# Rotating 32 x 3 images by 90 degrees: one group of four slabs in 32 KB rows, and a first transfer of 1 MB

## The chip, the cores and the metric

The kernel runs on one core of a Trainium2 chip. The metric is the device time of one execution in microseconds (us): 123.2 us before the change, the median of three runs (122.94 to 123.29).

## The reference

```python
def setup_inputs():
    batch, c, h, w = 32, 3, 256, 256
    return {"x": np.random.randn(batch, c, h, w).astype(np.float32)}

def reference(x):
    return np.rot90(x, k=-1, axes=(-2, -1)).astype(np.float32)
```

Each of the 96 images of 256 x 256 floats is turned clockwise: out[i, j] = x[255 - j, i]. Nothing is calculated; 25.17 MB are read, rearranged and written.

## The kernel before

The input is seen as 24,576 rows of 256 floats (1 KB each), `rows_in`; the output likewise, `rows_out`. A **slab** is 2,048 rows, 8 images, 2 MB: 128 partitions times 16 rows. There are 12 slabs, and they are kept in six **pairs** of 4 MB. Each pair has its own tile `u` of 32 KB per partition, so all 24 MB lie in SBUF at once (192 KB per partition) and no buffer is used twice.

**Loads.** All go out from SP's queue, in program order, before any store. Pair 0 comes as two transfers of 2 MB, one per slab (line 55), each partition getting two rows of 8 KB; slab 1 is loaded first. Pairs 1 to 5 come as two transfers each (line 59), for every second partition: 64 partitions with two rows of 16 KB, one from each half of the pair, 2 MB apart in memory.

**Turning.** VectorE (DVE) transposes blocks of 32 x 32 elements, 2048 elements per partition to an instruction; access patterns on both sides do the rest of the rotation, negative steps included. A pair is turned in place. Since an instruction would overwrite what another has not read yet, `turn_pair` cuts the pair into four quarters (low and high half of the columns, low and high half of the rows): the first quarter is written to `spare[n % 2]`, one of two tiles in PSUM (line 78); the other three are written into the places that the quarter before set free (line 82); then ScalarE (ACT) copies the first quarter from `spare` to the place that is left, in two copies (line 84). Pair 0 has another layout: slab 1 is turned into both `spare` tiles, slab 0 into slab 1's place (`turn_slab`, line 65), and ACT copies the `spare` tiles into slab 0's place (line 70).

**Stores.** Two transfers of 2 MB for each pair (line 97), each from every second partition, in rows of 16 KB. They go out from SP's queue as well, so each one stands behind all the loads and behind the stores of the pairs before it.

The order of the work is set by the data: the framework puts in the semaphore waits. A transfer also waits for an earlier one whose semaphore it takes over (eight are in use). PSUM is read and written by DVE and ACT alone.

Of the kernel before, what the change touches and what calls it, by code (L numbers as in the profile page):

```python
# [1 line left out]

# [4 lines left out]


@with_exitstack  # L10
def kernel(
    ctx: ExitStack,
    tc: tile.TileContext,
    x: bass.AP,
    out: bass.AP,
):

    nc = tc.nc
    fp32 = mybir.dt.float32

    B, C, H, W = x.shape
    P = nc.NUM_PARTITIONS
    R = 16
    I = 2  # L30
    E = R * W
    n_slabs = B * C * H // (P * R)
    hw = R // 2

    rows_in = x.rearrange("b c h w -> (b c h) w")
    rows_out = out.rearrange("b c h w -> (b c h) w")

    def short(rows):
        return rows.rearrange("(n i p r) w -> n p i (r w)", i=I, p=P, r=R // I)

    def long(rows):
        return rows.rearrange("(n a i m r) w -> n i m a (r w)", a=2, i=I, m=P // I, r=R)

    ld_short, ld_long, st_long = short(rows_in), long(rows_in), long(rows_out)

    pairs = [
        ctx.enter_context(tc.tile_pool(name=f"pair{n}", bufs=1)).tile([P, 2, E], fp32, name=f"u{n}")
        for n in range(n_slabs // 2)
    ]
    psum = ctx.enter_context(tc.tile_pool(name="psum", bufs=1, space=bass.MemoryType.PSUM))  # L50
    spare = [psum.tile([P, E // 2], fp32, name=f"spare{h}") for h in range(2)]


    for s, home in ((1, 0), (0, 1)):
        nc.sync.dma_start(
            out=pairs[0][:, home].rearrange("p (i f) -> p i f", i=I), in_=ld_short[s])
    for n in range(1, len(pairs)):
        for i in range(I):
            nc.sync.dma_start(out=pairs[n][i::I], in_=ld_long[n, i])

    def turn_slab(src, dsts):
        s = src.rearrange("p (i r g c) -> p c r g i", i=I, r=R // I, c=R)
        for h, d in enumerate(dsts):
            d = d.rearrange("p (c k r) -> p c r k", c=hw, r=R // I)[:, :, ::-1, ::-1]
            nc.vector.transpose(out=d, in_=s[:, h * hw : (h + 1) * hw])  # L65

    turn_slab(pairs[0][:, 0], spare)
    turn_slab(pairs[0][:, 1], [pairs[0][:, 0, : E // 2], pairs[0][:, 0, E // 2 :]])
    for h in range(2):
        nc.scalar.copy(out=pairs[0][:, 1, h * E // 2 : (h + 1) * E // 2], in_=spare[h])  # L70

    def turn_pair(n):
        u = pairs[n]
        src = u.rearrange("p a (r g c) -> p c r g a", r=R, c=R)
        dst = u.rearrange("p i (c k r) -> p c r k i", c=R, r=R)[:, :, ::-1, ::-1, :]
        held = spare[n % 2]
        low, high = slice(0, hw), slice(hw, R)
        nc.vector.transpose(  # L78
            out=held.rearrange("p (i c k r) -> p c r k i", i=I, c=hw, r=hw)[:, :, ::-1, ::-1, :],
            in_=src[:, low, low])  # L80
        for c, r in ((low, high), (high, high), (high, low)):
            nc.vector.transpose(out=dst[:, c, r], in_=src[:, c, r])  # L82
        for i in range(I):
            nc.scalar.copy(  # L84
                out=u[:, i, : E // 2].rearrange("p (c r) -> p c r", r=R)[:, :, hw:],
                in_=held[:, i * E // 4 : (i + 1) * E // 4].rearrange("p (c r) -> p c r", r=hw))

    for n in range(1, len(pairs)):
        turn_pair(n)
    for n in range(len(pairs)):  # L90
        for a in range(2):
            if n == 0:

                st = rows_out[: 2 * P * R].rearrange("(s i m r) w -> i m s (r w)", s=2, i=I, r=R)[a]
            else:
                st = rows_out.rearrange("(n a i m r) w -> n a m i (r w)", a=2, i=I, m=P // I, r=R)[n, a]
            nc.sync.dma_start(out=st, in_=pairs[n][a::2])


# [1 line left out]
_INS = ['x']  # L101
_OUTS = [((32, 3, 256, 256), 'float32')]


# [23 lines left out]
```

## Time and profile before

The profiled execution took 122.98 us, of which 121.2 us are the span that the profile shows.

| what | value |
|---|---|
| median of three runs | 123.2 us |
| profiled execution | 122.98 us |
| its span | 121.2 us |
| data moved | 50.33 MB, mean 415 GB/s over the span |
| transfers | 12 loads and 12 stores, 2 MB each |
| DVE, ACT busy | 86.6 us, 14.5 us |
| last store issued | 101.14 to 103.11 us (two issues) |

The lines of groups give: code line, engine, operation, target <- source with partitions x elements and type, count, then total busy time, mean duration of one in ns, and after the second bar the idle time of the engine before them with what ended most of it. Slices are forty equal parts of the span; the DMA digits are the mean busy share of the 16 DMA engines in tenths (9 is 90% or more). Lines of stretches give the window, its length, busy time of DVE, ACT and POOL with counts, the clock of TensorE (not used here), DMA share and GB/s.

### The profile page before, as it was taken

To read this page: it belongs to the slowest core of one execution; us is meant where nothing else is said; L and a number is where in the kernel's file an instruction comes from. 1 tells how busy PE (TensorE), PEld (TensorE's weight loads), DVE (VectorE), ACT (ScalarE), POOL (GpSimd) and SP (SyncE) were. 2 spreads that over 40 slices of the span, in tenths; PEclk is the share of its full clock that TensorE was granted. 3 is DMA by queue.
4 is the path that set the end of the run, shared out by engine and by line. 5 is a ranking of instruction groups with operands and counts; after the bars stand their busy time and mean duration, and the time that the engine had idled before them with its cause. 6 is when DMAs were issued, how large, how long until landed. Compare 5 with 4: busy or idle time off the path is not lost.

```text
span 121.2 us, 125 instructions
## 1 busy us (share of the span) xinstructions
DVE 86.6 (71%) x24; ACT 14.5 (12%) x13; POOL 0.2 (0%) x4
## 2 busy tenths in 40 slices
DVE  0029999619999999999999999999999970000000
ACT  0000400380000330005000060000600023000000
POOL 0000000000000000000000000000000000000000
DMA  4999999999999999999999999999999999999994
GB/s 87 403 419 433 465 433 433 427 427 433 433 411 422 416 427 433 433 433 433 422 433 433 433 433 433 433 433 433 433 433 433 433 427 427 433 433 433 433 433 184
DMA packets 3713, 50.33 MB, mean 415 GB/s; under 512 B 385, under 2 KB 385, under 8 KB 385
## 3 DMA queue, kind: packets, MB, share of 16 engines
q1 hardware_dynamic: 3712, 50.33, 97.9%
q14 instruction: 1, 0.00, 0.0%
HBM read 25.17 MB, written 25.17 MB: 415 GB/s over the span
## 4 chain that ended last, share of the span: by engine, by line
DVE 60%; issue 13%; DMA 6%; ACT 2%; ACTq 1%
DVE u L82 33%; DVE spare L78 15%; DVE u L65 6%; DMA u<-in_x_dram 6%; DVE spare L65 6%; ACT u L70 2%; ACT u L84 1%; ACTq L123 1%
## 5 line engine op out<-in xcount | busy, mean ns | idle before, releaser
L82 DVE STREAM_TRANSPOSE u<-u 128x2048 f32<-128x2048 f32 x15 | 54.3, 3619 | 0.5
L78 DVE STREAM_TRANSPOSE spare<-u 128x2048 f32<-128x2048 f32 x5 | 17.9, 3574 | 3.7 <-ACT u L70 3.7
L84 ACT COPY u<-spare 128x1024 f32<-128x1024 f32 x10 | 9.6, 1014 | 64.6 <-DVE u L82 64.6
L65 DVE STREAM_TRANSPOSE spare<-u 128x2048 f32<-128x2048 f32 x2 | 7.1, 3585 | 8.3 <-DMA u<-in_x_dram 8.3
L65 DVE STREAM_TRANSPOSE u<-u 128x2048 f32<-128x2048 f32 x2 | 7.8, 3986 | 0.0
L70 ACT COPY u<-spare 128x2048 f32<-128x2048 f32 x2 | 3.6, 1869 | 8.7 <-DVE u L65 8.7
L70 ACT ACT_TABLE_LOAD x1 | 1.3, 1283 | 13.3 <-DMA u<-in_x_dram 13.3
L112 POOL MEMSET const-bfloat16-1.0<- 128x1 bf16 x1 | 0.1, 101 | 0.0
L112 POOL MEMSET const-uint8-127<- 128x1 uint8 x1 | 0.1, 101 | 0.0
L112 POOL MEMSET const-float32-0.0<- 128x1 f32 x1 | 0.1, 98 | 0.2 <-issue 0.2
L112 POOL MEMSET const-float32-1.0<- 128x1 f32 x1 | 0.1, 98 | 0.0
## 6 DMA issues: line engine op xcount, KB each, us to landing
u<-in_x_dram SPq DMA_DIRECT2D x12, 2048.0 KB, 31.1
out_dram<-u SPq DMA_DIRECT2D x12, 2048.0 KB, 28.3
```

The source lines that it names most:

```text
L65: nc.vector.transpose(out=d, in_=s[:, h * hw : (h + 1) * hw])
L70: nc.scalar.copy(out=pairs[0][:, 1, h * E // 2 : (h + 1) * E // 2], in_=spare[h])
L78: nc.vector.transpose(out=held.rearrange("p (i c k r) -> p c r k i", i=I, c=hw, r=hw)[:, :, ::-1, ::-1, :], in_=src[:, low, low])
L82: nc.vector.transpose(out=dst[:, c, r], in_=src[:, c, r])
L84: nc.scalar.copy(out=u[:, i, : E // 2].rearrange("p (c r) -> p c r", r=R)[:, :, hw:], in_=held[:, i * E // 4 : (i + 1) * E // 4].rearrange ...
L112: nc = _bacc.Bacc("TRN2", target_bir_lowering=False, num_devices=1)
L123: with _tile.TileContext(nc) as tc:
```

## The change

- The six pairs become five **groups** of 2, 2, 4, 2 and 2 slabs (`sizes`). The group of four is one tile of 64 KB per partition.
- Group 0 is loaded in three transfers instead of two: slab 1 in two of 1 MB, each with one row of 8 KB per partition, then slab 0 in one of 2 MB as before.
- A group with `I` slabs is loaded in `I` transfers of 2 MB, each for every `I`-th partition. For the group of four this means 32 partitions with two rows of 32 KB, which lie 4 MB apart in memory. The groups of two are loaded as before.
- `turn_pair` becomes `turn_group`. With four slabs each quarter is turned by `T` = 2 instructions of 2048 elements, so the group has eight transpositions, two of them into both `spare` tiles, and its quarter is copied back by eight copies of 512 elements (two `spare` tiles, four slabs). In place, each instruction now writes to four places 16 KB apart.
- The first quarter of group 1 goes to a new tile `extra` in SBUF (8 KB per partition); the group of four uses both `spare` tiles, group 3 `spare[0]` and group 4 `spare[1]`.
- The stores keep their size and shape: 2 MB from every second partition, in rows of 16 KB. The group of four has four of them, for its first two slabs and then for its last two.

```diff
     nc = tc.nc
     fp32 = mybir.dt.float32
     B, C, H, W = x.shape
     P = nc.NUM_PARTITIONS
     R = 16
-    I = 2
     E = R * W
-    n_slabs = B * C * H // (P * R)
     hw = R // 2
+    low, high = slice(0, hw), slice(hw, R)
     rows_in = x.rearrange("b c h w -> (b c h) w")
     rows_out = out.rearrange("b c h w -> (b c h) w")
-    def short(rows):
-        return rows.rearrange("(n i p r) w -> n p i (r w)", i=I, p=P, r=R // I)
-
-    def long(rows):
-        return rows.rearrange("(n a i m r) w -> n i m a (r w)", a=2, i=I, m=P // I, r=R)
-
-    ld_short, ld_long, st_long = short(rows_in), long(rows_in), long(rows_out)
-
-    pairs = [
-        ctx.enter_context(tc.tile_pool(name=f"pair{n}", bufs=1)).tile([P, 2, E], fp32, name=f"u{n}")
-        for n in range(n_slabs // 2)
+    sizes = (2, 2, 4, 2, 2)
+    first = [sum(sizes[:n]) for n in range(len(sizes))]
+    groups = [
+        ctx.enter_context(tc.tile_pool(name=f"group{n}", bufs=1)).tile([P, s, E], fp32, name=f"u{n}")
+        for n, s in enumerate(sizes)
     ]
     psum = ctx.enter_context(tc.tile_pool(name="psum", bufs=1, space=bass.MemoryType.PSUM))
     spare = [psum.tile([P, E // 2], fp32, name=f"spare{h}") for h in range(2)]
+    extra = ctx.enter_context(tc.tile_pool(name="extra", bufs=1)).tile([P, E // 2], fp32, name="extra")
+
+    def rows_of(rows, n):
+        return rows[first[n] * P * R : (first[n] + sizes[n]) * P * R]
-    for s, home in ((1, 0), (0, 1)):
-        nc.sync.dma_start(
-            out=pairs[0][:, home].rearrange("p (i f) -> p i f", i=I), in_=ld_short[s])
-    for n in range(1, len(pairs)):
+    ld = rows_of(rows_in, 0).rearrange("(s i p r) w -> s i p (r w)", s=2, i=2, p=P)
+    home = [groups[0][:, s].rearrange("p (i f) -> p i f", i=2) for s in range(2)]
+    for i in range(2):
+        nc.sync.dma_start(out=home[0][:, i], in_=ld[1, i])
+    nc.sync.dma_start(out=home[1], in_=ld[0].transpose([1, 0, 2]))
+    for n in range(1, len(sizes)):
+        I = sizes[n]
+        ld = rows_of(rows_in, n).rearrange("(a i m r) w -> i m a (r w)", a=2, i=I, m=P // I)
         for i in range(I):
-            nc.sync.dma_start(out=pairs[n][i::I], in_=ld_long[n, i])
+            nc.sync.dma_start(
+                out=groups[n].rearrange("p s f -> p (s f)").rearrange("p (a f) -> p a f", a=2)[i::I],
+                in_=ld[i])
     def turn_slab(src, dsts):
-        s = src.rearrange("p (i r g c) -> p c r g i", i=I, r=R // I, c=R)
+        s = src.rearrange("p (i r g c) -> p c r g i", i=2, r=R // 2, c=R)
         for h, d in enumerate(dsts):
-            d = d.rearrange("p (c k r) -> p c r k", c=hw, r=R // I)[:, :, ::-1, ::-1]
+            d = d.rearrange("p (c k r) -> p c r k", c=hw, r=R // 2)[:, :, ::-1, ::-1]
             nc.vector.transpose(out=d, in_=s[:, h * hw : (h + 1) * hw])
-    turn_slab(pairs[0][:, 0], spare)
-    turn_slab(pairs[0][:, 1], [pairs[0][:, 0, : E // 2], pairs[0][:, 0, E // 2 :]])
+    u = groups[0]
+    turn_slab(u[:, 0], spare)
+    turn_slab(u[:, 1], [u[:, 0, : E // 2], u[:, 0, E // 2 :]])
     for h in range(2):
-        nc.scalar.copy(out=pairs[0][:, 1, h * E // 2 : (h + 1) * E // 2], in_=spare[h])
+        nc.scalar.copy(out=u[:, 1, h * E // 2 : (h + 1) * E // 2], in_=spare[h])
-    def turn_pair(n):
-        u = pairs[n]
-        src = u.rearrange("p a (r g c) -> p c r g a", r=R, c=R)
-        dst = u.rearrange("p i (c k r) -> p c r k i", c=R, r=R)[:, :, ::-1, ::-1, :]
-        held = spare[n % 2]
-        low, high = slice(0, hw), slice(hw, R)
-        nc.vector.transpose(
-            out=held.rearrange("p (i c k r) -> p c r k i", i=I, c=hw, r=hw)[:, :, ::-1, ::-1, :],
-            in_=src[:, low, low])
+    def turn_group(n, held):
+        I = sizes[n]
+        T = I // 2
+        K = W // (R * T)
+        u = groups[n].rearrange("p s f -> p (s f)")
+        src = u.rearrange("p (a t r g c) -> p t c r g a", a=2, t=T, r=R, c=R)
+        dst = u.rearrange("p (i c k t r) -> p t c r k i", i=I, c=R, k=K, t=T)[:, ::-1, :, ::-1, ::-1, :]
+        for t in range(T):
+            nc.vector.transpose(
+                out=held[t].rearrange("p (i c k r) -> p c r k i", i=I, c=hw, k=K)[:, :, ::-1, ::-1, :],
+                in_=src[:, t, low, low])
         for c, r in ((low, high), (high, high), (high, low)):
-            nc.vector.transpose(out=dst[:, c, r], in_=src[:, c, r])
-        for i in range(I):
-            nc.scalar.copy(
-                out=u[:, i, : E // 2].rearrange("p (c r) -> p c r", r=R)[:, :, hw:],
-                in_=held[:, i * E // 4 : (i + 1) * E // 4].rearrange("p (c r) -> p c r", r=hw))
+            for t in range(T):
+                nc.vector.transpose(out=dst[:, t, c, r], in_=src[:, t, c, r])
+        back = u.rearrange("p (i c k t r) -> p t i c k r", i=I, c=R, k=K, t=T)[:, ::-1]
+        for t in range(T):
+            kept = held[t].rearrange("p (i c k r) -> p i c k r", i=I, c=hw, k=K)
+            for i in range(I):
+                nc.scalar.copy(out=back[:, t, i, low, :, high], in_=kept[:, i])
-    for n in range(1, len(pairs)):
-        turn_pair(n)
-    for n in range(len(pairs)):
-        for a in range(2):
-            if n == 0:
+    for n, held in enumerate(([extra], spare, [spare[0]], [spare[1]]), 1):
+        turn_group(n, held)
-                st = rows_out[: 2 * P * R].rearrange("(s i m r) w -> i m s (r w)", s=2, i=I, r=R)[a]
-            else:
-                st = rows_out.rearrange("(n a i m r) w -> n a m i (r w)", a=2, i=I, m=P // I, r=R)[n, a]
-            nc.sync.dma_start(out=st, in_=pairs[n][a::2])
+
+    st = rows_of(rows_out, 0).rearrange("(s i m r) w -> i m s (r w)", s=2, i=2, m=P // 2)
+    for a in range(2):
+        nc.sync.dma_start(out=st[a], in_=groups[0][a::2])
+    for n in range(1, len(sizes)):
+        st = rows_of(rows_out, n).rearrange("(a i m r) w -> a m i (r w)", a=2, i=sizes[n], m=P // 2)
+        for i in range(0, sizes[n], 2):
+            for a in range(2):
+                nc.sync.dma_start(out=st[a][:, i : i + 2], in_=groups[n][a::2, i : i + 2])
```

## The prediction

> **What bounds the kernel now.** I read the page's head and its forty slices first, then the groups by line, then the waits, then stretches of the DMA stream.
>
> ```profile
> span 121.2 us, 125 instructions
> DVE 86.6 (71%) x24; ACT 14.5 (12%) x13; POOL 0.2 (0%) x4
> DMA  4999999999999999999999999999999999999994
> GB/s 87 403 419 433 465 433 433 427 427 433 433 411 422 416 427 433 433 433 433 422 433 433 433 433 433 433 433 433 433 433 433 433 427 427 433 433 433 433 433 184
> q1 hardware_dynamic: 3712, 50.33, 97.9%
> ```
>
> One queue keeps the 16 DMA engines busy for 97.9% of the span: only the first and the last slice have gaps. DVE is busy for 71%. The chain of waits names DVE for 60% of the span, but it ends when the last store is issued, at 103 us, and the data of that store waits in the queue for some 17 us more. So the bytes set the end: 25.17 MB in, then 25.17 MB out, in one unbroken line. Three things can move the time: the unfilled start, the rate, and a hole in the line.
>
> ```profile
> 0.00:2.00 2.00, 0.00 (x0) 0.00 (x0) 0.20 (x4) 1.00 0.20 29
> 5.00:12.00 7.00, 3.74 (x2) 0.00 (x0) 0.00 (x0) 1.00 1.01 428
> 14.00:57.00 43.00, 39.06 (x12) 7.20 (x7) 0.00 (x0) 1.00 1.01 428
> 62.00:118.00 56.00, 36.88 (x11) 5.78 (x6) 0.00 (x0) 1.00 1.01 433
> 119.90:121.20 1.30, 0.00 (x0) 0.00 (x0) 0.00 (x0) 1.00 0.00 0
> ```
>
> The last two columns are DMA share and GB/s. Loads in 8 KB rows (5 to 12 us) run at 428, loads in 16 KB rows (14 to 57) at 428, stores in 16 KB rows at 433. No data moves after 119.9. Counted back from there, the stores of the last four of the six pairs (16.78 MB at 433 = 38.8) begin at 81.1 us.
>
> ```profile
> L82 DVE STREAM_TRANSPOSE u<-u 128x2048 f32<-128x2048 f32 x15 | 54.3, 3619 | 0.5
> L78 DVE STREAM_TRANSPOSE spare<-u 128x2048 f32<-128x2048 f32 x5 | 17.9, 3574 | 3.7 <-ACT u L70 3.7
> L84 ACT COPY u<-spare 128x1024 f32<-128x1024 f32 x10 | 9.6, 1014 | 64.6 <-DVE u L82 64.6
> L65 DVE STREAM_TRANSPOSE u<-u 128x2048 f32<-128x2048 f32 x2 | 7.8, 3986 | 0.0
> L70 ACT COPY u<-spare 128x2048 f32<-128x2048 f32 x2 | 3.6, 1869 | 8.7 <-DVE u L65 8.7
> 13.27 1.28 ACT L70 ACT_TABLE_LOAD   x1 [13.27 <-DMA u<-in_x_dram]
> 23.23 3.63 ACT L70 COPY u<-spare 128x2048 f32<-128x2048 f32 x2 [8.67 <-DVE u L65]
> SPq L59 <- DMA u<-in_x_dram: 15.4, 4, 4.3
> ```
>
> The same 2048 elements per partition take 3619 ns written in place by L82 and 3986 ns by L65: the write pattern matters, by 10%.
>
> **The change part by part.** The sum is made on the profiled execution, 122.98 us: its span of 121.2 and 1.78 around it. That is 0.2 under the median of 123.2; at the end I carry the difference over to the median.
>
> *32 KB rows.* The 8.39 MB of the large group come in 256 rows instead of 512. At 428 they take 19.60 us. Bounds: the stores' 433 would make it 19.37, a gain of 0.23; the nearest step, from 8 to 16 KB rows, changed 428 into 428, a gain of nothing. A loss is not excluded, since each load now spans 32 partitions and its rows lie in two places 4 MB apart, not 2: the worst slice of loads past the start ran at 411, which makes it 20.41, a loss of 0.81. I take a gain of 0.10, between the two near rows.
>
> A rule of the Trainium skill speaks against this part: in "DMA: Bandwidth & Descriptors", section "Latency and other measured facts", copies lose rate when partitions step through HBM by large powers of two (164 GB/s at a 2 MiB pitch, 103 at 4 MiB). The pitch between this kernel's two rows per partition is 2 MB, and its loads run at 428 all the same. If the rule held for the step from 2 to 4 MB, the group would load at 428 x 103/164 = 269 and take 31.2 us, 11.6 longer, an estimate from that page; I go by the row.
>
> *The first transfer.* Before, 2 MB in 256 rows; after, 1 MB in 128, then 1 MB, then 2 MB: the same bytes, one more issue.
>
> ```profile
> 1.70:1.80 0.10, 0.00 (x0) 0.00 (x0) 0.00 (x0) 1.00 0.00 0
> 1.80:1.90 0.10, 0.00 (x0) 0.00 (x0) 0.00 (x0) 1.00 0.87 164
> 2.20:2.30 0.10, 0.00 (x0) 0.00 (x0) 0.00 (x0) 1.00 0.70 164
> 2.30:2.50 0.20, 0.00 (x0) 0.00 (x0) 0.00 (x0) 1.00 0.00 0
> 3.00:4.00 1.00, 0.00 (x0) 0.00 (x0) 0.00 (x0) 1.00 0.91 377
> ```
>
> The engines' first rows are spread over 1.8 to 2.3 us, and the full rate comes later. In this stretch and its neighbours 1.05 MB moved from 1.7 to 5.0; at 428 that takes 2.45 us, so the start wastes 0.85. This is the upper bound of the gain. If the spread of 0.5 us comes from handing out 256 rows, half the rows make it 0.25, and I take that gain. The other bound: nothing is gained, and the extra issue costs one issue of L55 (442 ns in the median). That issue is hidden, since 1 MB keeps the engines busy for 2.45 us; with that cover gone it would cost 0.44. On SP it delays the eleven loads behind it by 0.44, all of which already queue far ahead of the data. The first transposition still needs both halves of its slab, so DVE starts at about 8.2 as now.
>
> *SP.* Four loads now wait for an earlier landing (the last row of the groups above: the ninth to twelfth wait for the first to fourth). With thirteen loads five wait, and their first landings come earlier, after 1 MB. Stores keep their order behind all loads; every group's store stands behind the group before it, so one late group holds up all later ones.
>
> *DVE and ACT, and whether the line of stores stays closed.* Pair 0 is unchanged and ends at 23.20. The second group holds its first quarter in `extra`, so the wait of 3.7 us for L70's copies is gone: off the path, worth nothing, because next comes the large group, which needs four loads. They land at 13.27 + 12.58 MB / 428 = 42.7. The second group ends by 23.2 + 3.57 to 3.99 (its first write goes to SBUF now) + 3 x 3.62 = 38.1 at the latest, so DVE then idles for some 5 us. The large group: 2 x 3.57 + 6 x 3.62 = 28.9, ending at 71.6. Its copies: 2048 elements took 1869 ns and 1024 took 1014, so 0.835 ns each and 159 fixed; eight of 512 elements take 587 each, 4.7 together. All done at 76.3; by the code's order the first store needs six of them, 75.1. First data of a transfer came 0.97 after its issue began (0.73 to 1.70) and an issue of a store lasts 0.6; with 1.6 for both, on the safe side, store data is ready by 77.9 against 81.1 when the line would run dry. The margin is 3.2 us.
>
> The third large step: the next group's first write needs `spare[0]` free, that is, four copies, 2.4 us of DVE idle: 71.6 + 2.4 + 14.4 = 88.4, plus 2 copies 90.4, needed at 81.1 + 19.4 = 100.5. The last group: 102.8 plus copies 104.8, needed at 110.2. Both are covered, by some 8 and 4 us after the issue.
>
> What the trace doesn't show is the large group's write pattern: four places 16 KB apart, 128 bytes between neighbours, where L82 had two places and 64 bytes. Nearest rows: 3.57 and 3.99. At 3.99 the six in-place steps add 2.2 and the margin is still 1.0. So this part costs nothing, covered by the queue of stores.
>
> The Trainium skill's page "SBUF — State Buffer" ("Door 1: The DMA port swizzle") says that each access that crosses into another 16-byte line pays. All of these strides cross at every element, so by it they cost the same 3.62; the 3986 beside 3619 shows that the stride does matter here, and I keep 3.99 as the upper row.
>
> *Sum:* 122.98 - 0.10 - 0.25 = 122.63 for the profiled execution, a change of -0.35; on the median 122.85.
>
> **The rivals.**
>
> *A hole in the stores* (the slower side). If the eight transpositions of the large group take over 3.2 / 8 = 0.40 more each (4.0 in place), the engines run dry at 81 us, and each 0.1 beyond costs 0.8. For it: L65's 3986 lies just under that bound, and the pattern has wider strides than any seen. Against: L82's pattern already jumps 16 KB at every element and runs at 3619. With twice L65's excess, 0.74 each: 5.9 - 3.2 = 2.7, less the 0.35: 125.5.
>
> *The 32 KB rows load slower.* At 411: +0.81 - 0.25: 123.8. For it: only 32 partitions per transfer. Against: 128 and 64 partitions ran at the same 428.
>
> *Nothing arrives.* The rows are cut into 16 KB packets, or gain nothing, and the start is ruled by the first reads and not by the row count: 123.2. For it: 8 and 16 KB rows show one rate, and the later issues with 128 rows took longer (606 ns) than the first two with 256 (442).
>
> *The start is mended in full:* -0.85 - 0.10: 122.25.
>
> **How the numbers follow.** Forecast 0.50, its own range 122.5 to 123.1; hole 0.17; slower rows 0.08; nothing 0.18; start in full 0.07. About 0.3%, 0.37 us or 122.83 on the median, is what a measurement of this kernel can tell from no change. The forecast lies on that line: I give 0.30 of it to faster and 0.20 to same. With the full start faster has 0.37; rounded up for gains in both parts at once, 0.40. Same: 0.20 + 0.18 less that share, 0.35. Slower: hole and slower rows, 0.25. The range goes from 122.4 to 124.2: below lies most of the full start, above most of the hole.
>
> **What would show it.** Right: 256 fewer packets in the queue's line (not counting those of the one transfer more); the first rows spread over less than 0.5 us and the first 1 MB moved before 4.8; 428 or more between 23 and 42 us; DVE idle for about 5 us before the large group; no slice under 420 around 81 us; the last data at about 119.5. Wrong: in-place steps of the large group over 4.0 us with a dip of the DMA share near 81 (the hole), or a lower rate between 23 and 42 (slower rows).

## The result, and the profile after

The changed kernel took 123.5 us in the median of 21 runs (123.21 to 123.75), the kernel before 123.1 in as many (122.85 to 123.43). The ratio is 1.0034, 95% interval 1.0026 to 1.0042: slower by 0.4 us. The profiled execution of the changed kernel took 123.44 us with a span of 121.6.

The head of the page after, with the forty slices and the queue:

```profile
span 121.6 us, 130 instructions
DVE 87.4 (72%) x24; ACT 14.9 (12%) x17; POOL 0.2 (0%) x4
DMA  4999999998989899999999999999999999999993
GB/s 92 423 426 434 442 431 431 436 506 356 506 356 506 350 431 431 426 431 431 377 409 431 431 431 431 442 431 431 431 431 442 431 436 431 431 431 431 431 431 135
q1 hardware_dynamic: 3472, 50.33, 97.7%
```

The packets fell from 3712 to 3472: 256 rows fewer, and 16 completions more for the one transfer more. So the 32 KB rows are really moved as such. The 506 and 356 in turn from 24 to 42 us are these rows, whose bytes are counted where a row begins. Two slices stand out that have no counterpart before: 377 and 409, from 58 to 64 us. There the last load ends and the first store begins. I call this place **the turn**. The same stretches as before, with DMA share and GB/s last:

```profile
5.00:12.00 7.00, 3.88 (x2) 0.00 (x0) 0.00 (x0) 1.00 1.00 421
23.00:41.00 18.00, 14.91 (x5) 5.63 (x4) 0.00 (x0) 1.00 1.01 437
59.00:61.00 2.00, 2.00 (x2) 0.00 (x0) 0.00 (x0) 1.00 0.99 328
61.00:63.00 2.00, 2.00 (x1) 0.00 (x0) 0.00 (x0) 1.00 0.95 393
62.00:118.00 56.00, 38.06 (x11) 7.96 (x12) 0.00 (x0) 1.00 1.01 433
```

And the same stretches around the turn in the kernel before:

```profile
59.00:61.00 2.00, 1.97 (x2) 0.00 (x0) 0.00 (x0) 1.00 1.03 426
61.00:63.00 2.00, 2.00 (x1) 0.00 (x0) 0.00 (x0) 1.00 0.98 418
```

The share stays near 1 while the rate falls to 328: the engines are busy, and each packet takes longer (up to 1265 ns for 16 KB, where 611 to 615 is the rule). This is no hole. DVE and ACT by time, at the places that the prediction spoke of:

```profile
22.90 3.90 DVE L85 STREAM_TRANSPOSE extra<-u 128x2048 f32<-128x2048 f32 x1
42.29 7.08 DVE L85 STREAM_TRANSPOSE spare<-u 128x2048 f32<-128x2048 f32 x2 [4.28 <-DMA u<-in_x_dram]
49.40 21.91 DVE L90 STREAM_TRANSPOSE u<-u 128x2048 f32<-128x2048 f32 x6
71.34 3.03 ACT L95 COPY u<-spare 128x512 f32<-128x512 f32 x6 [2.68 <-DVE u L90]
72.94 3.61 DVE L85 STREAM_TRANSPOSE spare<-u 128x2048 f32<-128x2048 f32 x1 [1.63 <-ACT u L95]
```

The large group starts at 42.29 (42.7 was forecast), its six steps in place take 21.91 / 6 = 3.65 each, and its copies end at 74.4. The forecast's side of DVE and ACT holds within 2 us, and the line of stores is closed: 433 GB/s from 62 to 118.

**Where the 0.4 us went.** Windows of 2 us are too coarse for tenths, since a packet counts whole where it begins. The trace's packet records are finer: each transfer leaves 16 short packets of 4 bytes, one by each DMA engine, which I call its completions. The time from one transfer's completions to the next repeats to some ns while nothing changes. Worked out from these records (us; mean of the 16 engines, and the last engine; "second profile" is that of the changed kernel run again, below):

```
                               before     after      after, second profile
2 MB load, 16 KB rows           4.893      4.894      4.894      mean
2 MB load, 32 KB rows            -         4.855      4.857      mean
2 MB store                      4.862      4.862      4.862      mean
first data start at             1.82       1.74       1.73
first 2 MB complete at          7.64       7.49       7.50       mean
last load (the turn), mean      4.95       5.45       5.37
last load (the turn), last      4.89       5.65       5.53
spread of the 16 before it      0.56       0.45       0.53
last completion of all        120.06     120.44     120.39
```

The start is 0.15 us ahead, and four loads of the large group save 4 x 0.037 = 0.15 more. The last load then takes 0.50 us longer than before on the mean and 0.76 on the last engine (0.42 and 0.64 in the second profile). From there to the end every store takes 4.862 in both kernels. On the mean this makes -0.15 - 0.15 + 0.50 = +0.20 (0.18 by the completions of the last store); the last completion is 0.38 later, since the engines also stand further apart after the turn (0.82 us against 0.36) and the last of them sets the end. So in both profiles of the changed kernel the whole loss arises in one transfer, the last load, at the turn. Of the kernel before there is one profile.

### The profile page after: what moved, and what is told of

The parts are those of the page before. It is cut to its first block, busy times and chain, and to the rows that moved or that the text cites. A ratio compares the mean times of both kernels' runs of the same rounds, so it can differ in the third digit from the quotient of the medians.

```text
span 121.6 us, 130 instructions
## 1 busy us (share of the span) xinstructions
DVE 87.4 (72%) x24; ACT 14.9 (12%) x17; POOL 0.2 (0%) x4
## 2 busy tenths in 40 slices
DMA packets 3472, 50.33 MB, mean 414 GB/s; under 512 B 400, under 2 KB 400, under 8 KB 400
## 3 DMA queue, kind: packets, MB, share of 16 engines
q1 hardware_dynamic: 3472, 50.33, 97.7%
HBM read 25.17 MB, written 25.17 MB: 414 GB/s over the span
## 4 chain that ended last, share of the span: by engine, by line
DVE 42%; DMA 30%; issue 7%; SPq 4%; ACT 2%; ACTq 1%; DVEq 0%
DVE u L90 30%; DMA u<-in_x_dram 30%; DVE spare L85 12%; SPq L61 3%; ACT u L95 2%; ACTq L134 1%; SPq L55 1%; SPq L56 0%; DVEq L85 0%
## 5 line engine op out<-in xcount | busy, mean ns | idle before, releaser
L85 DVE STREAM_TRANSPOSE spare<-u 128x2048 f32<-128x2048 f32 x4 | 14.3, 3586 | 5.9 <-DMA u<-in_x_dram 4.3
L95 ACT COPY u<-spare 128x512 f32<-128x512 f32 (+1 forms) x12 | 8.0, 743 | 55.9 <-DVE u L90 55.9
L69 DVE STREAM_TRANSPOSE spare<-u 128x2048 f32<-128x2048 f32 x2 | 7.1, 3584 | 8.1 <-DMA u<-in_x_dram 8.1
L85 DVE STREAM_TRANSPOSE extra<-u 128x2048 f32<-128x2048 f32 x1 | 3.9, 3899 | 0.0
L95 ACT COPY u<-extra 128x1024 f32<-128x1024 f32 x2 | 2.0, 1043 | 11.3 <-DVE u L90 11.3
```

The lines of the kernel that those rows point to most:

```text
L85: nc.vector.transpose(out=held[t].rearrange("p (i c k r) -> p c r k i", i=I, c=hw, k=K)[:, :, ::-1, ::-1, :], in_=src[:, t, low, low])
L95: nc.scalar.copy(out=back[:, t, i, low, :, high], in_=kept[:, i])
```

## The experiments

All are compared with the kernel before on the same chip. Of each run one execution was profiled, so a loss at the turn is known from that one alone, while the ratios stand on 4 to 12 executions. The 59 to 61 us lines are stretches of the DMA stream as above.

**Which part of the change makes the turn dear.** The changed kernel again, the split of the first transfer alone in the kernel before, the large group alone, and the extra tile alone.

```diff
# e1_split: the kernel before, and
+    home = [pairs[0][:, s].rearrange("p (i f) -> p i f", i=I) for s in range(2)]
+    for i in range(I):
+        nc.sync.dma_start(out=home[0][:, i], in_=ld_short[1][:, i])
+    nc.sync.dma_start(out=home[1], in_=ld_short[0])
# e2_four: the changed kernel, and
-    for i in range(2):
-        nc.sync.dma_start(out=home[0][:, i], in_=ld[1, i])
+    nc.sync.dma_start(out=home[0], in_=ld[1].transpose([1, 0, 2]))
# e3_extra: the kernel before, and
-        held = spare[n % 2]
+        held = extra if n == 1 else spare[n % 2]
```

> The changed kernel once more, as the yardstick of this chip. Theory T (the loss sits where the queue turns from loads to stores, near 60 us): ratio about 1.003, the stretch 59 to 61 us below 350 GB/s again, loads of the large group at least as fast as before. Rival R (one accidental profile, the loss is elsewhere): the same ratio, but 59 to 61 us at 420 or more.

> The kernel before with the first 2 MB in two transfers of 1 MB, nothing else. If the split sets what the turn costs: ratio about 1.003 and 59 to 61 us below 350 GB/s. If the split only touches the start, as my prediction had it: 0.998 to 1.000 and 59 to 61 us at 420 or more.

> The changed kernel with the first slab in one transfer of 2 MB as before: the large group alone. If the 32 KB rows set what the turn costs: ratio about 1.003 and 59 to 61 us below 350 GB/s. If the split does: 0.998 to 1.000 and 420 or more there.

> The kernel before with the first quarter of pair 1 in an extra tile in SBUF: DVE runs 3.7 us ahead after 23 us, the transfers are the same. If what DVE and ACT do near 60 us sets what the turn costs: ratio 1.002 or more. If the queue alone does: 1.000.

Measured: changed kernel 1.0033 (1.002 to 1.0045), split alone 1.0027 (1.0017 to 1.0038), large group alone 1.0004 (0.9995 to 1.0013), extra tile 0.9999 (0.9991 to 1.0008). The stretch from 59 to 61 us in these four, in this order:

```profile
59.00:61.00 2.00, 2.00 (x2) 0.00 (x0) 0.00 (x0) 1.00 0.98 328
```

```profile
59.00:61.00 2.00, 1.97 (x2) 0.00 (x0) 0.00 (x0) 1.00 0.95 369
```

```profile
59.00:61.00 2.00, 2.00 (x2) 0.00 (x0) 0.00 (x0) 1.00 0.97 360
```

```profile
59.00:61.00 2.00, 1.97 (x2) 0.00 (x0) 0.00 (x0) 1.00 1.01 426
```

The split alone makes the kernel slower, though its stores are issued at the same times as in the kernel before, to 0.05 us. My expectation that only one of the two parts does it was too simple, and 369 and 360 lie between its two cases: by the completions the last engine loses 0.29 us at the turn with the split, 0.37 with the large group and 0.64 to 0.76 with both, against 4.89. The large group pays its 0.37 in part with the 0.15 that it saves, and comes out even. What DVE and ACT do near 60 us is not seen to play a part: with the extra tile the stores of the third and the fourth pair are issued 3.2 us earlier, and the time stays the same.

**The start, or one transfer more?** The split adds a 25th transfer. Splitting the second 2 MB, or both, tells these apart; two more runs take the first stores out of SP's queue.

```diff
# f1_split_second: the kernel before, and (f2_split_both: both slabs in rows, four transfers)
+    nc.sync.dma_start(out=home[0], in_=ld_short[1])
+    for i in range(I):
+        nc.sync.dma_start(out=home[1][:, i], in_=ld_short[0][:, i])
# f3_after_act: the changed kernel, and (f4_before_act: the kernel before, the same for pair 0)
-        nc.sync.dma_start(out=st[a], in_=groups[0][a::2])
+        nc.scalar.dma_start(out=st[a], in_=groups[0][a::2])
```

> The kernel before with the second 2 MB (slab 0) in two transfers of 1 MB and the first left whole: again 25 transfers, but the start is as before. Theory S (the start's shape sets how the engines meet the turn): ratio 0.999 to 1.001. Theory C (one transfer more ahead of the turn does it): 1.002 to 1.004 and 59 to 61 us under 400 GB/s.

> The kernel before with both slabs of pair 0 in transfers of 1 MB: 26 transfers, and the start of the changed kernel. Theory S: as with the first alone, 1.002 to 1.004. Theory C: if every further transfer adds, 1.005 or more; if it matters only whether their number is odd, 1.000.

> The changed kernel with the two stores of group 0 issued from ACT's queue, so that they run between the loads from 28 us on and the loads end some 10 us later. If the loss is the price of all engines turning from loads to stores at one moment: 0.997 to 0.999 of the kernel before (the turn is spread out, the faster 32 KB rows remain). If each change between reading and writing costs by itself: above 1.005.

> The kernel before with the two stores of pair 0 issued from ACT's queue, as in the run beside it. If turning at one moment costs: 0.999 to 1.000, since this kernel loses little there. If mixed reading and writing costs: above 1.003.

Measured: second split 1.0004 (0.9994 to 1.0013); both 1.0026 (1.001 to 1.0043). So the number of transfers plays no part, and neither does its being odd: by the ratios it is the split of the first transfer that costs. With both split the last engine loses 0.29 at the turn, as with the first alone. Two things make this less firm than it looks. The run with the second 2 MB split loses 0.15 at its turn as well, in a profiled execution of 123.38 us, 0.31 above its median. And the twelve executions with both split go from 123.02 to 123.86 us: the fastest lose nothing, so the loss differs from one execution to the next and is not fixed by the kernel alone.

The stores from ACT's queue were a miss. The kernel before came to 1.0043 (1.0027 to 1.0059). Its final turn had become free (the last load took 4.862 on the mean and on the last engine), but while stores ran between the loads, from 32 to 52 us, everything was slower: three loads and two stores took 25.34 us there, where five times 4.89 would be 24.45. The first line is this kernel, the second the kernel before:

```profile
23.00:41.00 18.00, 14.20 (x5) 3.63 (x2) 0.00 (x0) 1.00 1.01 406
```

```profile
23.00:41.00 18.00, 14.20 (x5) 3.63 (x2) 0.00 (x0) 1.00 1.00 428
```

The Trainium skill, "DMA: Bandwidth & Descriptors", section "Issuing engines are not separate DMA queues", says that transfers issued by several engines run on the same 16 DMA engines and interleave, so that this saves issue time alone. Here it was no gain but a loss: 406 against 428.

The changed kernel with these stores came to 1.0232 (1.0213 to 1.0251), for another reason. The loads of the large group ended 8 us later, DVE began it at 50.35, and the stores were not ready when the line needed them:

```profile
79.00:82.00 3.00, 1.37 (x2) 2.60 (x6) 0.00 (x0) 1.00 0.69 295
82.00:85.00 3.00, 2.97 (x2) 0.44 (x1) 0.00 (x0) 1.00 0.51 213
```

Here the DMA share itself falls, to 0.51. This is how the hole that my prediction feared looks. It also shows how large the margin is. The copies of the large group ended at 82.43 instead of 74.37, and its first store took 2.0 us longer than 4.862 on the last engine and 2.6 on the mean, so the line ran again some 1.5 us after the copies. In the changed kernel the stores ahead of it are complete at 81.1 (mean) to 81.5 us (last engine), which leaves a margin of some 5.3 to 5.6 us, an estimate from these two runs; I had 3.2.

**Does it matter how far apart the engines arrive?** In the first profiles, a narrow spread of the 16 completions went with a dear turn (0.40 to 0.53 us ahead of it, against 0.56 and 0.68 in the kernel before and the one with the extra tile). A small load of 8 rows of 8 KB, read into the `extra` tile and used by nothing, puts more work on some engines; an early store makes the queue turn twice.

```diff
# g1_split_skew: e1_split, and after the loads of pair 0 (g2_after_skew: the changed kernel, the same)
+    nc.sync.dma_start(out=extra[:8], in_=rows_in[: 8 * hw].rearrange("(p r) w -> p (r w)", r=hw))
# g3_before_early: the kernel before, the loads of pair 5 behind the first store (g4_split_early: e1_split, the same)
+    nc.sync.dma_start(out=st0[0], in_=pairs[0][0::2])
+    for i in range(I):
+        nc.sync.dma_start(out=pairs[5][i::I], in_=ld_long[5, i])
```

> The kernel with the split alone (1.0027), plus one small load after group 0: 8 rows of 8 KB, which puts 0.31 us of extra work on some of the 16 engines and none on the others, so that they stand further apart at the turn. Theory A (the turn is dear because the split lets the engines arrive close together): the turn gets cheaper by about what the load costs, ratio 1.000 to 1.003. Theory B (how far apart they stand plays no part): the load's 0.31 us is added, 1.004 to 1.006.

> The changed kernel (1.0033) with the same small load. Theory A: 1.000 to 1.003, and the stretch 59 to 61 us better than 328 GB/s. Theory B: 1.005 to 1.007.

> The kernel before with the first store put in SP's queue ahead of the last two loads: the queue changes from loads to stores twice and back once. If each change costs what it costs at 60 us in this kernel (under 0.1 us): 1.000 to 1.002. If stores between loads are dear as in the run with ACT's queue: 1.003 or more.

> The kernel with the split alone, with the same early store. If each change from loads to stores costs the split kernel 0.3 us: 1.005 or more. If only the first store ever costs (a first touch of the output or the like): 1.002 to 1.003, with the loss at some 52 us and none at the second change.

Measured: 1.0078 (1.0062 to 1.0094), 1.0067 (1.0053 to 1.0081), 1.0022 (1.0013 to 1.0031) and 1.0058 (1.0043 to 1.0073). By the ratios alone theory B would seem to win in the second, nothing fits the first, the third lies between its two cases, and the fourth in that of a fixed price for each change. The trace shows something else. In both kernels with the small load the turn is free: the last load takes 4.90 on the last engine. The loss has moved to the small load. But the small load did not do what I put it in for: ahead of the turn the engines stand 0.50 and 0.54 us apart, hardly more than without it (0.49 with the split alone, 0.45 and 0.53 in the changed kernel). So these two runs do not decide between A and B. The first of them, around the small load and at the turn:

```profile
10.00:12.00 2.00, 2.00 (x2) 0.00 (x0) 0.00 (x0) 1.00 1.06 451
12.00:14.00 2.00, 2.00 (x1) 0.24 (x1) 0.00 (x0) 1.00 1.09 299
14.00:16.00 2.00, 1.97 (x2) 1.05 (x1) 0.00 (x0) 1.00 1.02 434
59.00:61.00 2.00, 1.97 (x2) 0.00 (x0) 0.00 (x0) 1.00 1.04 442
```

Right after the small load 16 packets of 16 KB take 1124 to 1455 ns, and from the completions of the load ahead of it to those of the 2 MB behind it 5.83 us pass on the mean instead of 4.89: 0.93 lost for a load whose 8 rows are worth 0.31 (an estimate: 8 KB at a sixteenth of 428 GB/s). The Trainium skill, "DMA: Bandwidth & Descriptors", section "Why a DMA increments its semaphore by 16 and not by 1", has a transfer run on the largest number of engines, at most 16, that divides the slowest dimension on both sides, so 8 here. The trace agrees: 408 short packets, which is 25 x 16 for the other transfers and 8 for this one.

```profile
DMA packets 3744, 50.40 MB, mean 412 GB/s; under 512 B 408, under 2 KB 408, under 8 KB 408
```

The early store in the split kernel, around the first place where its queue turns to stores and around the second:

```profile
48.00:50.00 2.00, 1.97 (x2) 0.00 (x0) 0.00 (x0) 1.00 0.93 393
50.00:52.00 2.00, 2.00 (x1) 0.00 (x0) 0.00 (x0) 1.00 0.99 328
52.00:54.00 2.00, 1.97 (x2) 0.00 (x0) 0.00 (x0) 1.00 0.92 393
66.00:68.00 2.00, 1.97 (x2) 0.00 (x0) 0.00 (x0) 1.00 0.96 410
```

The first change to stores costs 0.82 us on the last engine, the second 0.05. In the kernel before the first costs 0.25 and the second nothing (its last load takes 4.863); there the way back costs some 0.19 on the last engine, in the store between (4.979) and the load behind it (4.965). So a change from loads to stores has no fixed price, and neither has the kernel: in these two runs the price is higher at the first one and nearly nothing after. A price of the first store as such (a first touch of the output) is not the reason, since the first store costs nothing in the two kernels with the small load. The engines had been 0.22 us apart ahead of the first change in the split kernel, and 0.88 apart after it.

What happens to the engines is seen in the completions. Each row holds the 16 of one transfer, sorted, in ns after the first of them: the last but one load (ahead of the turn) and the last store.

```
before              ahead   0  35 233 250 256 282 287 300 306 314 316 319 421 438 554 562
                    last    0  55  70  86  87 102 119 125 135 188 219 225 246 302 357 365
after               ahead   0  87 187 207 207 216 223 228 233 236 273 309 336 414 438 446
                    last    0  20  65 133 161 180 181 194 607 623 708 743 771 796 805 821
split alone         ahead   0  17 195 196 196 222 227 255 260 263 271 280 316 318 344 492
                    last    0  10 195 227 248 253 256 295 556 557 581 650 670 720 754 770
split, small load   ahead   0  39  39  58  95 121 149 162 196 260 343 368 408 427 493 500
                    last    0  39  39  59  97 150 171 197 198 261 340 366 403 434 491 507
```

In these two dear turns two sets of eight engines come out, 0.41 us apart in the changed kernel and 0.26 in the split one, and keep that distance to the end. The same is seen in the second profile of the changed kernel and in the split kernel with the early store (0.32 and 0.37). It is no rule: behind the turn of the large group alone, which lost 0.37, the completions show no gap in the middle (17 ns). In the free turn with the small load the pattern hardly changes.

**Is it a price that is paid once?** This was my theory P: eight engines must fall behind the other eight once, and the first place that forces it pays. Four runs try it: the small load ahead of everything, a smaller one in the middle, and the small load in the kernel before.

```diff
# h1_four_small_first: e2_four, and ahead of the first load
+    nc.sync.dma_start(out=extra[:8, :512], in_=rows_in[: 8 * 2].rearrange("(p r) w -> p (r w)", r=2))
# h2_after_small_first: the changed kernel, 8 rows of 8 KB ahead of the first load
# h3_after_tiny: the changed kernel, 8 rows of 2 KB after the loads of group 0
# h4_before_skew: the kernel before, 8 rows of 8 KB after the loads of pair 0
```

> The large group with an unsplit first slab (1.0004), and ahead of everything a load of 8 rows of 2 KB, which only 8 of the 16 engines carry. Theory P (eight engines have to fall behind the other eight once, and the queue pays for it at the first place that forces it; at the turn if nothing has before): the small load sets them apart where the start is unfilled anyway, the turn is free, and the 0.15 us of the 32 KB rows remain: 0.998 to 1.000. Rival Q (the turn's loss has its own cause): 1.001 to 1.002.

> The changed kernel (1.0033) with a load of 8 rows of 8 KB ahead of everything. P: turn free, up to 0.31 us for the rows: 0.999 to 1.002. Q: the rows are added, 1.004 to 1.006.

> The changed kernel with a load of 8 rows of 2 KB after group 0 (the 8 KB rows there gave 1.0067). P: the setting apart is paid there instead of at the turn, the rows themselves cost 0.08 us: 1.003 to 1.005, with no loss at the turn. Q (what was paid there was the price of a load on eight engines, by its bytes): a quarter of the 0.9 us, so 1.005 to 1.006 if the turn still loses, 1.000 to 1.001 if not.

> The kernel before with the load of 8 rows of 8 KB after pair 0, as in the split kernel that came to 1.0078 with it. P: where the engines stand apart already, only the rows cost: 1.002 to 1.004. Q: the load costs 0.9 us here too: 1.007 to 1.008.

Measured: 1.0041 (1.0029 to 1.0053), 1.0063 (1.0047 to 1.0079), 1.0036 (1.0024 to 1.0048), 1.0097 (1.0077 to 1.0116). Theory P falls: of the four ratios only the third lies in its range, and there the turn is as dear as before, where P has it free. In the kernel before, whose turn is cheap anyway, the small load costs 1.22 us on the mean and 1.8 on the last engine: that price is the load's own, there too with packets of up to 1652 ns behind it. Ahead of everything it neither makes the turn free (0.27 and 0.82 lost on the last engine) nor is it hidden: the first 2 MB are complete at 8.13 and 8.03 us instead of 7.56 and 7.49. The one of 2 KB rows leaves the turn as dear as it was (0.53). What stands is less: where an event in mid-stream had cost 0.8 us or more (the small load of 8 KB rows in three kernels, one of them with a cheap turn anyway; the early store in the split kernel), the next change to stores was cheap. Why is not shown.

**What of the split it is, and the partitions at the turn.**

```diff
# k1_split_parts: the kernel before, first 2 MB in two transfers by partitions
+    for j in range(2):
+        nc.sync.dma_start(out=home[0][j::2], in_=ld_short[1][j::2])
# k2_after_odd: the changed kernel, and
-    for a in range(2):
+    for a in (1, 0):
         nc.sync.dma_start(out=st[a], in_=groups[0][a::2])
```

> The kernel before with its first 2 MB in two transfers of 1 MB, but divided by partitions (even ones, then odd ones, two rows of 8 KB each) and not by rows. If a first transfer of 1 MB is what makes the turn dear: 1.002 to 1.004, as with the split by rows (1.0027). If it is the order of rows, one to a partition: 0.999 to 1.001.

> The changed kernel (1.0033) with the stores of group 0 in the other order, odd partitions first, so that the last load and the first store use the same partitions. If the turn is dear because neighbours of different partitions meet there: 0.999 to 1.001. If not: 1.003 to 1.004 and 59 to 61 us below 400 GB/s.

Measured: 1.0034 (1.0022 to 1.0046) and 1.0025 (1.0013 to 1.0037). The first looks like the split by rows and is not: its first data come at 2.24 us, since its issues are longer (0.7 us each), and DVE starts at 8.64 instead of 8.26.

```profile
0.73 1.41 SPq L56 DMA_DIRECT2D u<-in_x_dram  x2
8.64 3.61 DVE L66 STREAM_TRANSPOSE spare<-u 128x2048 f32<-128x2048 f32 x1 [8.64 <-DMA u<-in_x_dram]
```

The first 2 MB are complete 0.34 us later than in the kernel before, the last completion comes 0.37 later. That is its loss; at the turn its last engine loses 0.04 (0.12 on the mean). So, by the one profile of each, the same ratio has two causes in two kernels, and a 1 MB transfer at the start isn't enough to make the turn dear. The second kernel's turn stays dear (0.89 on the last engine, 311 GB/s from 59 to 61 us): that the last load and the first store use different partitions is not the reason.

## Why the prediction was wrong

The forecast was 122.85 us, faster, in a range of 122.4 to 124.2. The measured 123.5 lies inside the range and on the other side of no change.

- **The step that failed** is the premise: "25.17 MB in, then 25.17 MB out, in one unbroken line. Three things can move the time: the unfilled start, the rate, and a hole in the line." There is a fourth: the turn, where the engines go from loads to stores. No term of my sum stood for it. It cost 0.64 to 0.76 us on the last engine with the change and nothing before (0.42 to 0.50 more on the mean), more than the whole loss of 0.4. The profile before gave no sign of it: 426 and 418 GB/s from 59 to 63 us.
- **The first transfer** was put at a gain of 0.25 and gave 0.11: the first 2 MB were complete, on the mean of the engines, at 7.36 to 7.62 us in ten kernels with the split by rows, mean 7.51, and at 7.54 to 7.78 in seven without, mean 7.62. "If the spread of 0.5 us comes from handing out 256 rows, half the rows make it 0.25" was the wrong mechanism: with the first transfer whole, the large group alone had its first 16 rows begin within 1.81 to 1.99 us, and the second profile of the changed kernel, with half the rows, within 1.73 to 2.57. (The 1.70 that the prediction gives for the first data is 1.82 in the packet records, and its "No data moves after 119.9" means that no packet begins later; the last is complete at 120.06.) By the ratios this part is also the one that makes the kernel slower (1.0027 alone, against 1.0004 for the large group), and I had looked for its effect at the start alone.
- **The 32 KB rows** were put at a gain of 0.10; they gave 0.15 (0.037 in each of four transfers). A gain between the two near rows was right, if half as large again. Rows 4 MB apart in memory load no slower than rows 2 MB apart: the group's loads took 4 x 4.855 = 19.4 us, where the estimate from the Trainium skill's rule on row pitches was 31.2. That rule is stated for the pitch from one partition to the next, which is 32 KB in these loads, so it did not bear on this case.
- **DVE and ACT at nothing, covered by the queue of stores**: right. The copies of the large group were done at 74.4 us and its first store was issued then, where I had 75.1 to 76.3. The new write pattern costs 3.65 us, near the lower row that I had. `extra` in SBUF took 3.90, inside its bounds.
- **The rivals.** The hole did not come. The run in which the loads were 8 us late shows that it exists, and puts the margin at 5.3 to 5.6 us, not 3.2. "Slower rows" gave the right sign for the wrong reason: its bound of 0.81, taken from the worst slice of loads, happened to be near the loss at the turn; that is luck.

Of the signs that I had named, 256 packets fewer, 428 GB/s or more from 23 to 42 us, an idle DVE ahead of the large group (4.28 us) and no dip near 81 us came. The first 1 MB by 4.8 us (5.02) and the last data at 119.5 (120.4) did not.

Nothing tried beats the kernel before. The large group with the first transfer whole is equal to it (1.0004).

**What stays open:** why packets take up to twice as long at the turn in some executions, and how a split at the start can tell there, more than 50 us later. That the split works by way of the turn rests on single profiles, and turns without it lost 0.15 and 0.25 as well (second 2 MB split; early store in the kernel before). Narrow spreads go with dear turns, but not strictly: 0.22 us cost 0.82 in two kernels, 0.45 cost 0.76, while 0.56 cost nothing in the kernel before and 0.55 cost 0.53 in another. A spread of 0.50 and 0.54 cost nothing behind the small load. Which engine a packet belongs to is not visible in these records, and no run changed their order alone.

## What to carry to other kernels

When one queue is busy from end to end, look at its seams too: the first packets and the place where loads give way to stores. A share near 1 with a lower GB/s in a short stretch is a loss that no wait and no idle engine shows. A change elsewhere in such a queue can be paid for at its next seam, as here with both parts of the change, so compare the whole line transfer by transfer, and don't take equal ratios for equal causes.

## What the runs showed of the hardware

- The 16 engines keep their distances to some ns through a phase of equal transfers: 0.44 to 0.45 us apart over the last five loads of the changed kernel, 0.82 in every one of its stores.
- A load that only 8 engines carry is dear between full ones: 64 KB cost 0.9 us in the changed kernel and in the split one, 1.2 in the kernel before, most of it in the packets of the transfer behind it. With rows of 2 KB it cost 0.1.
- Stores issued from ACT's queue that ran at the same time as loads from SP's lowered what both moved together: 406 GB/s instead of 428.
- 2 MB loads in 16 KB rows took 4.893 us for most of the phase ahead of the stores, but 4.862, as stores do, behind the first stores (four loads in the kernel before with stores from ACT's queue, the first load behind the early store in the split kernel). So 428 against 433 GB/s does not come from the direction alone. In 32 KB rows the loads took 4.855.
- After the hole the engines stood 0.15 to 0.17 us apart, and five stores there took 4.90 to 4.93 us; in the other runs, 0.33 us apart and more, stores took 4.862. This is one run.
- Issues of the same 1 MB differ by shape: 0.43 us for 128 partitions with one row each, 0.7 for 64 with two.
